# A hybrid decoder block on one core: stores moved from ScalarE's queue to SyncE's, operands made under a cap, and a recurrence paced at 9.0 products per half

## The chip, the cores and the metric

The kernel runs on one core of one Trainium2 chip. The metric is the device time of one execution in microseconds (us); the kernel before took 1485.11 us, the median of three runs (1483.97 to 1486.83). Everything is in float32. To reach that precision on TensorE, each product is made of three matmuls of fp32r parts: an operand is split into a high part (a cast on ScalarE) and a low part (source minus high part, on VectorE), and high x high, high x low and low x high are summed.

## The reference

```python
proj = x @ w_in                       # (1024, 1024) @ (1024, 7168)
q, f_pre, i_val, o_gate, pool_v, gate_a, gate_b = split(proj)
f = lb + (1 - lb) * sigmoid(f_pre);  k = 1 - f
o = hgrn2_chunked(silu(q) * 128**-0.5, k, i_val, log(f))   # 8 heads of 128, S_t = diag(f_t) S_{t-1} + k_t v_t^T
o = o * rsqrt(mean(o*o) + eps) * g * sigmoid(o_gate)
a = o @ w_a
b = per_group_linear(causal_mean(pool_v, windows 2,4,8,16) - pool_v) * pool_scale
x = LN(alpha * x + (sigmoid(gate_a) * a + sigmoid(gate_b) * b) @ w_out)
x = LN(alpha * x + (relu(x @ w_up) ** 2) @ w_down)
```

The sequence has 1024 tokens, the model 1024 columns, the MLP 4096.

## The kernel before

Every large matrix product is computed blockwise in a 2 x 2 scheme with seven products in place of eight: two output column blocks of 128 form a pair, tokens and input columns are halved, and seven products (p1 to p7 of `pair_items` and `pair`) of sums of blocks give the four output blocks. One such product is 12 matmuls of 128 x 512.

The program has these stages: the values `i_val` in rows (lines 400 to 575), the stage called `flow` here (lines 610 to 1320), the product with `w_a` and the merging of the two branches (lines 1322 to 1400), `w_out` with the first layer norm, `w_up`, and `w_down` with the second layer norm. The change touches `flow` alone.

`flow` walks through a list of 176 products (called items): 24 pairs of seven, in the order that the table `ORDER` gives (inputs of a head, output gates, pooled columns, gates), and twice four items of the pooling's small linear map, also of 12 wide matmuls each (`products`, line 898). Behind each item three things are written:

- its evacuation (`evac`): a copy from PSUM on ScalarE (`copied`, L740) or an addition on VectorE (`added`, L743). What is done with the finished block (a sigmoid and a store, for the gates) is put off by one item (`later`, `soon`);
- the making of a weight operand for a later item (`Make.high`, cast L686; `Make.low`, subtraction L689). Some operands are sums of blocks and need a VectorE operation first (`pre`: L714, L720, L721). Ten `w` tiles allow five operands to be held. `beat` makes one; then, in `while (m := next_make()): at_once(m)`, all others that have a free place are made;
- one turn of the generator `recurrence`. It works through 16 halves of heads (512 tokens of one head). In turn 0 of a half TensorE gets the outputs of the half before, the transposes of the keys (L1031) and the scores (L1038, L1049); turn 4 has more of TensorE; the elementwise preparation of the next half (`prepare`, six pieces, the last of which ends with L1022 to L1024) fills the turns between. `PER_HALF = 9.5` lets halves take 9 and 10 turns in alternation, rounded.

The pooled means (`mean`, L853 to L860) are queued as `jobs`, of which one to three are done per item. Finished gates and other blocks are written to DRAM and read again by the `w_a` stage. In `flow`, the order on TensorE, VectorE, ScalarE and SyncE is as written (`manual_schedule`); a scheduler places the instructions of the following stage between and behind. SyncE issues nearly all loads and most stores (queue SP in the profile); 48 stores stand on ScalarE's queue (16 output gates, L804; 16 gates a, L822; 16 pooled results, L924). Each engine works through its own queue in order, so an instruction that waits holds up all behind it. For PSUM there are four banks for the seven products of a pair; the accumulating product p6 needs the copy of p1 done, p5 that of p6, p4 that of p7.

In the `w_a` stage the first product needs the block of `w_a` (`loaded_blocks`, L225), its cast (L126) and the heads' outputs (`o_jobs`, splits L131 and L132).

Of the kernel before, what the change touches and what calls it, by code (L numbers as in the profile page):

```python
# [26 lines left out]
HALO = 16  # L27
LINE = 16
NW = 10
PER_HALF = 9.5  # L30
TURN_BACK = 4
TURNS_AHEAD = 3
MANY_JOBS = 4
# [18 lines left out]
def tile_hybrid_block(  # L52
# [18 lines left out]
    nc = tc.nc  # L71
# [58 lines left out]
    def split_into(t, src):  # L130
# [9 lines left out]
        out=cmask, in_=cmask, compare_op=ALU.is_ge, fill=0.0, base=0,  # L140
# [444 lines left out]
    gad = [[dram(f"ga{j}_{u}") for u in range(2)] for j in range(8)]  # L585
    pbd = [[dram(f"pb{j}_{u}") for u in range(2)] for j in range(8)]
# [32 lines left out]
    with tc.tile_pool(name="tmp", bufs=1, side="right", reuse_waits="tile") as tmp:  # L619
# [178 lines left out]
        def output_gates(h):  # L798

            def take(dst, src=False):  # L800
                def put(t):
                    s = c_late() if src else t
                    A.activation(s, t, AF.Sigmoid)
                    nc.scalar.dma_start(out=dst, in_=s)  # L804
                return put

            return pair_items(
                3 * D + h * P, 3 * D + (h + 1) * P, (c_soon, c_late, c_late),
                (take(ogd[h][0]), take(ogd[h + 1][0], True), take(ogd[h][1]), take(ogd[h + 1][1])),
            )  # L810

        def gates(j):

            p = []

            def fetch():
                p[:] = [loaded(pbd[j][u], lambda: tt("x")) for u in (1, 0)]

            def take_a(u):
                def put(t):  # L820
                    A.activation(t, t, AF.Sigmoid)
                    nc.scalar.dma_start(out=gad[j][u], in_=t)  # L822
                return put

            def take_b(u, src):
                def put(t):
                    s = c_late() if src else t
                    A.activation(s, t, AF.Sigmoid)

                    def finish():  # L830
                        V.tensor_mul(p[1 - u], p[1 - u], s)
                        nc.sync.dma_start(out=pbd[j][u], in_=p[1 - u])
                    later(finish)
                return put

            return pair_items(
                5 * D + j * P, 6 * D + j * P, (c_soon, c_late, c_late),
                (take_a(0), take_b(0, True), take_a(1), take_b(1, False)), fetch,
            )

        def pooled(g):

            j, win = 2 * g, WINDOWS[g]
# [48 lines left out]
            def take_12(ps):  # L892
# [6 lines left out]
            xw, yw, items = pair_items(  # L899
                4 * D + j * P, 4 * D + (j + 1) * P,  # L900
                (lambda: room(0, 0), lambda: room(0, 1), lambda: room(1, 1)), (take_11, take_12, take_21, lambda _: None),
            )
# [7 lines left out]
            def products(u):  # L910

                ms, ps = [part(i, u) for i in range(2)], [None, None]

                def product():
                    for i in range(2):
                        w = slice(i * P, (i + 1) * P)
                        ps[i] = ps_tile()
                        mm3(ps[i], [(mw.w[0][:, k, w], mw.w[1][:, k, w], *ms[k].w) for k in range(2)])

                def evac():  # L920
                    for i in range(2):
                        t = c_late()
                        A.activation(t, ps[i], AF.Copy, scale=pscale[:, j + i : j + i + 1])
                        nc.scalar.dma_start(out=pbd[j + i][u], in_=t)  # L924

                return Item(ms if u else [*ms, mw], product, evac)

# [295 lines left out]
        def flow(items, raws, turns, at_end):  # L1223

            makes = [m for item in items for m in item.makes]
            slots = [m for m in makes if m.slot]
            place = {m: i for i, m in enumerate(slots)}
            users = {}
            for item in items:
                for m in item.makes:  # L1230
                    users[m] = item
            state = dict(make=0, load=0)

            def free(m):
                if not m.ready():
                    return False
                if not m.slot or place[m] < NW // 2:
                    return True
                return users_of(slots[place[m] - NW // 2]).issued

            def users_of(m):
                return m.reader or users[m]

            def loads():
                while state["load"] < len(raws):
                    n = state["load"]
                    if n >= 3 and not raws[n - 3].done:
                        return
                    raws[n].load(n)
                    state["load"] += 1  # L1250

            def next_make():
                if state["make"] < len(makes) and free(makes[state["make"]]):
                    state["make"] += 1
                    return makes[state["make"] - 1]

            def at_once(m):
                m.high()
                m.low()
                loads()  # L1260

            def beat(m):
                now = list(soon)
                soon.clear()
                for do in now:
                    do()
                if m:
                    m.high()
                next(turns, None)
                for _ in range(min(len(jobs), 1 + len(jobs) // MANY_JOBS, 3)):  # L1270
                    jobs.pop(0)()
                if m:
                    m.low()
                    loads()
                if state["make"] < len(makes) and makes[state["make"]].ready():
                    makes[state["make"]].before()
                    loads()

            loads()
            for i, item in enumerate(items):  # L1280
                while state["make"] < len(makes) and any(m.w is None for m in item.makes):
                    m = next_make()
                    assert m, (i, len(jobs))
                    at_once(m)
                if i == 0:
                    while (m := next_make()):
                        at_once(m)
                item.product()
                item.issued = True
                item.evac()  # L1290
                if i in at_end:
                    jobs.extend(at_end[i])
                m = next_make()
                beat(m)
                while (m := next_make()):
                    at_once(m)
            while soon or jobs:
                beat(None)
            for _ in turns:
                pass  # L1300
# [3 lines left out]
        with tc.manual_schedule(engines={mybir.EngineType.PE, mybir.EngineType.DVE, mybir.EngineType.Activation, mybir.EngineType.SP}):  # L1304
            items, raws, pools = [], [], []
# [12 lines left out]
            n = len(items)  # L1318
# [121 lines left out]
    with tc.tile_pool(name="wo", bufs=1, side="right", reuse_waits="tile") as mp:  # L1440
        st1 = [None] * 8
        g1, b1 = ln_params(lambda: f(act_tile()).rearrange("p a b -> p (a b)"), ln1_g, ln1_b)
        for k2 in range(0, KT, 2):
            raw = raw_rows(w_out, k2, 1)
            for k in range(2):
                n = len(wo)
# [240 lines left out]
    for b in range(NBLK):  # L1687
# [3 lines left out]
        if last:  # L1691

            for ring in (dh, dw):
                t = fw.tile([P, M, 2, HALF], F32R, tag="draw", name=nm("dx"), bufs=2)
# [65 lines left out]
```

## Time and profile before

| what | value |
|---|---|
| median of three runs | 1485.11 us (1483.97 to 1486.83) |
| the profiled execution | 1482.73 us |
| its span, first to last instruction | 1480.8 us |
| granted TensorE clock, mean | 0.992 |
| TensorE busy | 1437.0 us (97%) |
| VectorE busy | 1120.1 us (76%) |
| ScalarE busy | 767.3 us (52%) |
| DMA, mean rate | 148 GB/s |

Busy time of TensorE counts from the start of a matmul to its modelled end. Matmuls overlap: one of 128 x 512 is shown with some 0.39 us, and the next starts 0.23 us later. An idle time of TensorE in the profile is therefore some 0.16 us shorter than the delay that it stands for. The profile names for each idle time the instruction that ended it, as "line of the waiting one <- engine, tile and line of what it waited for". Line numbers are those of the kernel before; in the changed kernel they are one higher up to line 1278, seven higher behind the loop.

### The profile page before, as it was taken

To read this page: it belongs to the slowest core of one execution; us is meant where nothing else is said; L and a number is where in the kernel's file an instruction comes from. 1 tells how busy PE (TensorE), PEld (TensorE's weight loads), DVE (VectorE), ACT (ScalarE), POOL (GpSimd) and SP (SyncE) were. 2 spreads that over 40 slices of the span, in tenths; PEclk is the share of its full clock that TensorE was granted. 3 is DMA by queue.
4 is the path that set the end of the run, shared out by engine and by line. 5 is a ranking of instruction groups with operands and counts; after the bars stand their busy time and mean duration, and the time that the engine had idled before them with its cause. 6 is when DMAs were issued, how large, how long until landed. Compare 5 with 4: busy or idle time off the path is not lost.

```text
span 1480.8 us, 20562 instructions
## 1 busy us (share of the span) xinstructions
PE 1437.0 (97%) x7377; PEld 1190.3 (80%) x7377; DVE 1120.1 (76%) x1822; ACT 767.3 (52%) x1397; POOL 90.9 (6%) x260
## 2 busy tenths in 40 slices
PE   9999999999999989996999999999999999999997
PEld 7888888788778778785888888888888888888886
DVE  5957888778977887757986589666666787777978
ACT  5544665765665466554542347555555533343435
POOL 0002111111111011000002100000000100000000
PEclk9999999999999999998999999999999999999999
DMA  7232241432243245559564134444464774545322
GB/s 249 79 114 86 79 135 44 141 130 86 83 161 108 64 156 159 171 174 324 177 209 167 43 129 163 142 150 150 157 227 171 272 274 133 166 131 179 132 71 114
DMA packets 164454, 218.43 MB, mean 148 GB/s; under 512 B 10976, under 2 KB 92416, under 8 KB 164352
## 3 DMA queue, kind: packets, MB, share of 16 engines
q1 hardware_dynamic: 155504, 197.96, 40.1%
q10 hardware_dynamic: 7696, 14.96, 2.8%
q0 software_dynamic: 1152, 4.19, 0.9%
q8 instruction: 58, 0.95, 0.3%
q14 instruction: 44, 0.36, 0.1%
HBM read 149.96 MB, written 67.11 MB: 147 GB/s over the span
## 4 chain that ended last, share of the span: by engine, by line
PE 83%; DVE 9%; ACT 3%; DMA 2%; issue 2%; SPq 0%; ACTq 0%; DVEq 0%
PE ps_pj L209 14%; PE ps_pj L211 13%; PE ps_pj L212 13%; PE ps_pj L1643 4%; PE ps_pj L1642 4%; PE ps_pj L1641 4%; PE ps_pj L113 2%; PE ps_pj L115 2%; PE ps_pj L114 2%; DVE x L853 1%; PE ps_tr L1643 1%; PE ps_tr L1642 1%; PE ps_tr L1641 1%; DVE w L689 1%; PE ps_sc L209 1%
## 5 line engine op out<-in xcount | busy, mean ns | idle before, releaser
L209 PE MATMUL ps_pj<-act,w 128*128 128x512 f32 x1068 | 422.8, 396 | 28.2 <-ACT w L126 12.4
L211 PE MATMUL ps_pj<-act,w 128*128 128x512 f32 x1068 | 417.5, 392 | 0.5 <-DVE act L132 0.5
L212 PE MATMUL ps_pj<-act,w 128*128 128x512 f32 x1068 | 416.8, 391 | 0.0
L209 PEld LDWEIGHTS ps_pj<-act,w 128*128 128x128 f32 x1068 | 201.9, 189 | 76.9 <-ACT c L740 15.8
L212 PEld LDWEIGHTS ps_pj<-act,w 128*128 128x128 f32 x1068 | 201.8, 189 | 42.9
L211 PEld LDWEIGHTS ps_pj<-act,w 128*128 128x128 f32 x1068 | 201.9, 189 | 41.6 <-DVE act L132 0.9
L1603 ACT CAST act<-act 128x1024 fp32r<-128x1024 f32 x66 | 66.9, 1051 | 108.7 <-issue 35.0
L686 ACT CAST w<-t 128x512 fp32r<-128x512 f32 x96 | 59.6, 621 | 82.3 <-DVE t L714 34.2
L689 DVE TENSOR_TENSOR w<-t,w 128x512 fp32r<-128x512 f32 x96 | 65.6, 683 | 39.0 <-ACT w L686 38.2
L1643 PE MATMUL ps_pj<-act,act 128*128 128x512 f32 x240 | 92.9, 389 | 0.0
L1642 PE MATMUL ps_pj<-act,act 128*128 128x512 f32 x240 | 92.9, 389 | 0.0
L1641 PE MATMUL ps_pj<-act,act 128*128 128x512 f32 x240 | 92.4, 389 | 0.0
L1604 DVE TENSOR_TENSOR act<-act,act 128x1024 fp32r<-128x1024 f32 x66 | 79.2, 1218 | 17.0 <-ACT act L1603 17.0
L689 DVE TENSOR_TENSOR w<-raw,w 128x512 fp32r<-128x512 f32 x72 | 48.5, 685 | 45.6 <-ACT w L686 44.6
L126 ACT CAST w<-t 128x512 fp32r<-128x512 f32 x74 | 46.0, 622 | 63.7 <-PE ps_pj L211 40.4
L127 DVE TENSOR_TENSOR w<-raw,w 128x512 fp32r<-128x512 f32 x71 | 48.5, 688 | 35.8 <-ACT w L126 34.7
L126 ACT CAST w<-raw 128x512 fp32r<-128x512 f32 x71 | 43.9, 622 | 55.9 <-PE ps_pj L211 29.9
L127 DVE TENSOR_TENSOR w<-t,w 128x512 fp32r<-128x512 f32 x74 | 50.7, 686 | 18.2 <-ACT w L126 18.2
L743 DVE TENSOR_TENSOR c<-c,ps_pj 128x512 f32<-128x512 f32 x64 | 43.6, 681 | 17.7 <-PE ps_pj L212 17.7
L1642 PEld LDWEIGHTS ps_pj<-act,act 128*128 128x128 f32 x240 | 45.0, 188 | 9.4
L1641 PEld LDWEIGHTS ps_pj<-act,act 128*128 128x128 f32 x240 | 45.0, 188 | 9.4
L1643 PEld LDWEIGHTS ps_pj<-act,act 128*128 128x128 f32 x240 | 45.0, 188 | 9.3
(413 smaller groups left out, 2923.6 us busy)
## 6 DMA issues: line engine op xcount, KB each, us to landing
h<-c SPq DMA_DIRECT2D x106, 256.0 KB, 2.2
raw<-in_w_in_dram SPq DMA_DIRECT2D x96, 256.0 KB, 3.3
act<-h SPq DMA_DIRECT2D x78, 256.0 KB, 2.9
draw<-in_w_down_dram SPq DMA_DIRECT2D x16, 1024.0 KB, 8.1
raw<-in_w_up_dram SPq DMA_DIRECT2D x30, 512.0 KB, 4.0
hf<-h SPq DMA_DIRECT2D x34, 256.0 KB, 2.9
og<-c ACTq DMA_DIRECT2D x16, 256.0 KB, 2.1
v<-v SPq DMA_DIRECT2D x16, 256.0 KB, 3.7
```

Source lines behind the costliest of these rows:

```text
L126: A.copy(hi, src)
L127: V.tensor_sub(lo, src, f(hi))
L209: PE.matmul(ps, wh[:, k], th, start=first and k == 0, stop=False, skip_group_check=True)
L211: PE.matmul(ps, wh[:, k], tl, start=False, stop=False, skip_group_check=True)
L212: PE.matmul(ps, wl[:, k], th, start=False, stop=k == CH - 1, skip_group_check=True)
L686: A.copy(self.w[0], self.src())
L689: V.tensor_sub(self.w[1], self.src(), f(self.w[0]))
L1603: A.copy(hi, src)
L1604: V.tensor_sub(lo, src, f(hi))
L1641: PE.matmul(ps, hh[:, w], wh, start=fresh and n == 0, stop=False, skip_group_check=True)
L1642: PE.matmul(ps, hh[:, w], wl, start=False, stop=False, skip_group_check=True)
L1643: PE.matmul(ps, hl[:, w], wh, start=False, stop=n == M - 1, skip_group_check=True)
```

## The change

Three edits in `flow`. The 48 stores move from `nc.scalar` to `nc.sync`. `PER_HALF` is 9.0, so that each half takes nine turns. And behind an item at most one operand is made beside that of `beat`, and only while fewer than four of the items that follow have all their operands (`MADE_AHEAD`).

```diff
-PER_HALF = 9.5
+PER_HALF = 9.0
+MADE_AHEAD = 4
...
-                    nc.scalar.dma_start(out=dst, in_=s)
+                    nc.sync.dma_start(out=dst, in_=s)
...
-                    nc.scalar.dma_start(out=gad[j][u], in_=t)
+                    nc.sync.dma_start(out=gad[j][u], in_=t)
...
-                        nc.scalar.dma_start(out=pbd[j + i][u], in_=t)
+                        nc.sync.dma_start(out=pbd[j + i][u], in_=t)
...
+            def ahead(i):
+                n = i + 1
+                while n < len(items) and all(m.w is not None for m in items[n].makes):
+                    n += 1
+                return n - i - 1
...
                 m = next_make()
                 beat(m)
-                while (m := next_make()):
+                if i + 1 < len(items) and ahead(i) < MADE_AHEAD and (m := next_make()):
                     at_once(m)
```

The number of instructions on each engine stays the same, but for 48 DMA issues that change from ScalarE to SyncE. The last turn of the recurrence is written behind item 175, the last one, in the kernel before, and behind item 167 in the changed one.

The first place is SyncE's queue around the end of `flow`. In the rows, `s` and `o` are sums and outputs of heads in DRAM (L1139 to L1147: the last half's), `pb` the pooled branch, `q`, `f` and `c` loads of heads' outputs, `raw<-in_w_a_dram` the blocks of `w_a`; raw_7062 is the block that the first product behind `flow` needs. Before:

```order
L832 DMA pb_1_961<-x_6931 128x512
L599 DMA q_7010<-s_0_970 128x512
L599 DMA f_7012<-s_1_971 128x512
L832 DMA pb_0_960<-x_6933 128x512
L1147 DMA s_3_977<-og_6830 128x512
L599 DMA q_7032<-s_2_972 128x512
L599 DMA gb_7195<-pb_0_946 128x512
L599 DMA f_7034<-s_3_973 128x512
L599 DMA gb_7217<-pb_0_950 128x512
L225 DMA raw_7062<-in_w_a_dram 128x4x256
```

Now:

```order
L1141 DMA s_3_969<-tA_6453 128x512
L1142 DMA og_6654<-o_0_912 128x512
L1148 DMA s_3_977<-og_6654 128x512
L600 DMA gb_7195<-pb_0_946 128x512
L600 DMA gb_7217<-pb_0_950 128x512
L226 DMA raw_7062<-in_w_a_dram 128x4x256
L226 DMA raw_7063<-in_w_a_dram 128x4x256
L226 DMA raw_7462<-in_w_a_dram 128x4x256
L833 DMA pb_1_959<-x_6780 128x512
L823 DMA ga_1_943<-c_6778 128x512
```

The recurrence's last store (s_3_977) and with it the three loads of `w_a` stood behind the last item's store (pb_0_960 of pair 7 of the gates); now they stand ahead of the stores of pair 6 (pb_1_959), and one of the moved stores (ga_1_943) follows.

The second place is TensorE's queue at the same time: w_6901 (before) is the operand of the last item of `flow`, w_6873 and w_6893 (now) those of the third and second to last, and ps_pj_7078 the bank of the first product with `w_a`. Before:

```order
L209 MATMUL ps_pj_6861<-act_762,w_6901 128x512
L211 MATMUL ps_pj_6861<-act_762,w_6901 128x512
L212 MATMUL ps_pj_6861<-act_762,w_6902 128x512
L209 MATMUL ps_pj_7078<-act_6913,w_7070 128x512
L211 MATMUL ps_pj_7078<-act_6913,w_7070 128x512
L209 MATMUL ps_pj_7093<-act_6913,w_7074 128x512
```

Now:

```order
L210 MATMUL ps_pj_6878<-act_668,w_6873 128x512
L212 MATMUL ps_pj_6878<-act_668,w_6873 128x512
L213 MATMUL ps_pj_6878<-act_668,w_6874 128x512
L210 MATMUL ps_pj_7078<-act_6925,w_7070 128x512
L212 MATMUL ps_pj_7078<-act_6925,w_7070 128x512
L210 MATMUL ps_pj_6901<-act_460,w_6893 128x512
```

The products with `w_a` began behind the last item; now their first two matmuls stand two items earlier.

The third place is ScalarE's queue at the last of the four spots where a pooled map's items (L923, evacuation with a scale, and its store L924) are followed by a new pair, whose first product's copy is L740. Before:

```order
L923 ACTIVATE c_5707<-ps_pj_5693,prm 128x512
L924 DMA pb_1_959<-c_5707 128x512
L923 ACTIVATE c_5710<-ps_pj_5700,prm 128x512
L924 DMA pb_1_961<-c_5710 128x512
L686 CAST w_5714<-t_5687 128x512
L686 CAST w_5730<-t_5728 128x512
L740 COPY c_5747<-ps_pj_5734 128x512
```

Now:

```order
L924 ACTIVATE c_5798<-ps_pj_5784,prm 128x512
L924 ACTIVATE c_5801<-ps_pj_5791,prm 128x512
L687 CAST w_5805<-t_5778 128x512
L741 COPY c_5831<-ps_pj_5818 128x512
L687 CAST w_5833<-t_5816 128x512
```

Two stores and one of two casts no longer stand between the pooled evacuations and the copy; the second cast comes behind it. At the other three such spots there is one cast in place of two as well; at two of them the copy has the recurrence's squares or scalings (L1105, L1113) ahead of it now.

## The prediction

> **What bounds the kernel now.** I read the page's busy times first, then TensorE (PE) by stage, then who PE waited for.
>
> ```profile
> span 1480.8 us, 20562 instructions
> PE 1437.0 (97%) x7377; PEld 1190.3 (80%) x7377; DVE 1120.1 (76%) x1822; ACT 767.3 (52%) x1397; POOL 90.9 (6%) x260
> ```
>
> PE is idle for 1480.8 - 1437.0 = 43.8 us. The change removes no matmul, so it can only win from these waits and from time at a lowered clock. The stages, in the view by windows (busy us and count of each engine, then granted clock, DMA share, GB/s), are `flow`, the first moments of the `w_a` stage, its next 25 us, and the rest:
>
> ```profile
> 99.70:673.50 573.80, 557.41 (x3454) 462.99 (x3452) 447.03 (x869) 334.29 (x721) 68.86 (x211) 0.99 0.38 121
> 673.50:692.00 18.50, 6.10 (x15) 4.82 (x16) 12.92 (x21) 8.73 (x16) 0.00 (x0) 0.63 1.01 348
> 692.00:716.70 24.70, 24.10 (x108) 19.60 (x106) 21.51 (x35) 16.52 (x30) 0.00 (x0) 1.00 0.76 263
> 716.70:1480.80 764.10, 753.82 (x3352) 623.28 (x3352) 566.53 (x777) 359.04 (x547) 19.21 (x14) 1.00 0.46 158
> ```
>
> The change touches `flow` (16.4 us idle) and what follows at once (12.4 us and a clock of 0.63). The last row's code is the same in both kernels. Whom PE waited for:
>
> ```profile
> PE ps_pj L209 <- ACT w L126: 12.4, 1, 12.4
> PE ps_pj L209 <- ACT c L740: 12.0, 9, 3.6
> PE ps_pj L209 <- DVE f L743: 1.8, 2, 1.0
> ...
> PE ps_tr L1031 <- DVE tC L1022: 1.4, 2, 1.0
> ```
>
> One wait of 12.4 us at the seam, nine waits in `flow` for ScalarE's (ACT) copies out of PSUM, and little else.
>
> **The change, part by part.**
>
> *The seam.* PE's timeline there:
>
> ```profile
> 672.88 0.39 PE L211 MATMUL ps_pj<-act,w 128*128 128x512 f32 x1
> 673.11 0.39 PE L212 MATMUL ps_pj<-act,w 128*128 128x512 f32 x1
> 685.90 0.80 PE L209 MATMUL ps_pj<-act,w 128*128 128x512 f32 x1 [12.40 <-ACT w L126]
> ...
> 687.35 0.63 PE L211 MATMUL ps_pj<-act,w 128*128 128x512 f32 x1
> 687.77 0.63 PE L212 MATMUL ps_pj<-act,w 128*128 128x512 f32 x1
> ```
>
> Starts are 0.23 us apart ahead of the hole and 0.42 behind it. From start to start the hole is 12.79 us, 12.6 more than 0.23. The 15 matmuls counted up to 692.0 come at the halved clock and cost some 15 x 0.2 = 3.0 more. What PE waits for is the cast of the first block of `w_a`, and that waits for its load, which SyncE (SP) issues so late:
>
> ```profile
> 676.01 0.44 SPq L832 DMA_DIRECT2D pb<-x  x1
> 676.90 0.32 SPq L1147 DMA_DIRECT2D s<-og  x1
> ...
> 679.48 1.49 SPq L225 DMA_DIRECT2D raw<-in_w_a_dram  x3
> ```
>
> The loads stand behind the last item's store and the recurrence's last store, since the recurrence's last turn comes with the last item. With nine turns it comes with item 167, eight products or 8 x 12 x 0.23 = 22 us ahead of the end, and the order shows the three loads right behind its store, ahead of the stores of the second to last pair. A load of this kind lands in 5.6 us:
>
> ```profile
> raw<-in_w_a_dram SPq DMA_DIRECT2D x8, 512.0 KB, 5.6
> ga<-ga SPq DMA_DIRECT2D x16, 256.0 KB, 5.4
> og<-c ACTq DMA_DIRECT2D x16, 256.0 KB, 2.1
> pb<-x SPq DMA_DIRECT2D x16, 256.0 KB, 2.2
> ```
>
> So the blocks should be there over 10 us early, and PE's queue has the first matmuls of `w_a` two items ahead of the end of `flow`. The hole and the halved clock go: -15.6. What is late next is data. From 673.5 to 716.7 the transfers moved 18.5 x 348 + 24.7 x 263 KB per us, 12.9 MB. Of it 1.8 MB (three blocks of 512 KB and the last store of 256 KB) come earlier now; 11.1 MB stay. PE needs 43.2 - 15.6 = 27.6 us for the products in this stretch; 11.1 MB take 31.9 us at 348 GB/s and 42.2 at 263. By the first rate 4.3 us of wait come back, by the second 14.6. The faster rate is the one seen while PE waited for transfers, and some loads of heads' outputs get free behind the earlier stores too: I take 3.1. **Term: -12.5**, with ends -15.6 and -1.0.
>
> *At most two operands per product, stores off ACT.* Four of the nine waits for a copy come where a pooled map's items precede a new pair:
>
> ```profile
> 188.36 0.50 PE L209 MATMUL ps_pj<-act,w 128*128 128x512 f32 x1 [0.19 <-ACT c L740]
> ...
> 287.97 0.50 PE L209 MATMUL ps_pj<-act,w 128*128 128x512 f32 x1 [1.39 <-ACT c L740]
> ...
> 413.57 0.50 PE L209 MATMUL ps_pj<-act,w 128*128 128x512 f32 x1 [1.67 <-ACT c L740]
> ...
> 544.43 0.50 PE L209 MATMUL ps_pj<-act,w 128*128 128x512 f32 x1 [3.63 <-ACT c L740]
> ```
>
> Together 6.9 us. ACT's timeline shows why for the longest:
>
> ```profile
> 540.29 0.33 ACTq L924 DMA_DIRECT2D pb<-c  x1
> 540.66 0.62 ACT L686 CAST w<-t 128x512 fp32r<-128x512 f32 x1 [0.40 <-ACT c L923]
> 543.27 0.62 ACT L686 CAST w<-t 128x512 fp32r<-128x512 f32 x1 [2.00 <-DVE t L714]
> 543.80 0.58 ACT L740 COPY c<-ps_pj 128x512 f32<-128x512 f32 x1
> ```
>
> The second operand's cast waits 2.0 us for VectorE (DVE), and the copy stands behind it. The order puts this cast behind the copy now, and the two stores ahead of it, each 0.4 us from one ACT operation to the next, are gone. 2.0 + 0.6 + 0.8 = 3.4 of the 3.63 us go. The same is done at the other three spots. Two of them have the recurrence's squares in the way instead, but these come with PE's own extra work of that turn. The clock, by windows:
>
> ```profile
> 504.00:512.00 8.00, 6.17 (x21) 4.61 (x20) 7.65 (x18) 1.80 (x4) 0.00 (x0) 0.79 0.00 0
> 542.00:550.00 8.00, 5.57 (x17) 4.43 (x18) 7.32 (x15) 4.30 (x10) 0.00 (x0) 0.79 0.60 193
> 411.00:418.00 7.00, 5.33 (x23) 4.07 (x23) 6.13 (x13) 3.48 (x10) 0.10 (x1) 1.00 0.27 90
> ```
>
> Behind the wait of 3.63 us (second row) the clock loses 0.21 x 8 = 1.7 us; that goes with it. So up to 8.6 us can go; I take **-7**, with ends -8.6 and 0.
>
> The Trainium skill ("TensorE: Matmul & The Clock Gate", "What's actually happening") says that the clock is halved after an idle window of about 3.4 us. The trace differs: the row 504 to 512 shows the loss with an idle time of only 1.8 us in it, while 1.67 us (third row) cost none. By the page's rule every wait under 3.4 us that the new order makes is free of it; by the first row each of 1.8 us can cost 1.7, and only the wide end of my range has room for several.
>
> *The recurrence at 9.0.* Per product there is 9.5 / 9.0 = 1.056 times its work until item 167 and none behind. This costs only where DVE is full:
>
> ```profile
> 360.00:415.00 55.00, 50.82 (x290) 41.08 (x289) 50.14 (x107) 30.43 (x63) 8.25 (x23) 1.00 0.25 78
> 490.00:533.00 43.00, 38.70 (x231) 31.40 (x230) 39.78 (x86) 22.01 (x48) 5.37 (x17) 0.96 0.20 60
> ```
>
> These are the two stretches in which the pooled means of the wide windows are worked off; DVE is busy for 91% and 93%. Were all its work the recurrence's and every us of it on the path, it would add 0.056 x (50.1 + 39.8) = 5.0 us; elsewhere DVE has room (447 of 574 us over all of `flow`). The lower end is 0. I take half: **+2.5**. The other waits of `flow`, 16.4 - 6.9 = 9.5 us, I leave as they are; the halves start elsewhere among the pairs now, so each can move, and I give them 4 us either way.
>
> *48 stores on SP.* ACT is freed of 48 issues; outside of the spots above it has room (334 of 574 us), so nothing is counted. SP gets 48 issues of 0.3 to 0.4 us and waits at each until ACT has written the tile. Behind them stand raw loads, the recurrence's loads and the `pb` loads. How tight these are shows in who waited for a landing in `flow`:
>
> ```profile
> DVE og L1146 <- DMA og<-o: 3.2, 3, 1.7
> ...
> ACT w L686 <- DMA raw<-in_w_in_dram: 0.5, 1, 0.5
> ```
>
> A raw load was waited for once in 96; a store would have to hold SP for many products to be felt. L1146, the last sum of a head, is tight: its load is issued in turn 7, and nine turns leave it one product where ten left two. Four times up to 1.7 us on DVE, which PE feels only in a full stretch: **0**, with +2 in the range. The Trainium skill ("DMA: Bandwidth & Descriptors", "Issuing engines are not separate DMA queues") says that transfers interleave on the same 16 engines whoever starts them, and that several issuers save only issue time. The rows above agree: 2.1 us from ACT and 2.2 from SP to landing. By it the move as such brings nothing but ACT's time, and the sum has nothing else for it.
>
> **Sum:** -12.5 - 7 + 2.5 = -17 us against the profiled execution's 1482.7 (span 1480.8 and 1.9 around it), so 1465.7. The median of the runs is 1485.1, 2.4 above that execution; set off from it the forecast is **1468.1 us**.
>
> **The rivals.**
>
> *The transfers become the seam's bound.* For: 348 GB/s at a share of 1.01 in the row from 673.5, and 5.4 us to landing for `ga<-ga`. Against: a part of that rate was the late loads themselves. At 263 GB/s the seam's gain is 1.0: -1.0 - 7 + 2.5, 1479.6.
>
> *DVE is the bound in the full stretches and the waits only move.* For: 93% busy. The gains at the four spots are eaten by DVE's lag: -12.5 + 0 + 5.0 = -7.5, 1477.6.
>
> *Slower: PE waits for the last piece of `prepare` at the start of each half.* Place: the transposes L1031 of turn 0. With ten turns the last piece has a spare product, with nine it is written one product ahead of them, for all halves and not about every other one. It decides when DVE is over one product (2.7 us) behind at a half's end. At 2.7 us for 15 halves it costs 40 us, so 1468.1 + 40 = 1508; at a third of that the gain is nearly gone (1481). Against: halves of nine turns are there already, and the whole wait at L1031 was 1.4 us.
>
> *The change does not do what it says:* the loads of `w_a` are held by something else, such as space that the recurrence's tiles free, or PE, with two `w_a` matmuls ahead of its last items, stops there instead. Then the hole only moves: -7 + 2.5, 1480.6.
>
> *Better:* the smaller waits go as well (9.5 us and 1.7 of clock, half of it): 1462.5; with all, 1456.9.
>
> **How the numbers follow.** Forecast (1464 to 1474) 0.55, better 0.11, transfers 0.10, DVE 0.11, hole only moved 0.05, slower by L1031 0.08. A measurement of this kernel can tell about 0.2%, 3 us, from no change; below 1482.1 is faster. Faster are the first four (0.87) and 0.02 of the hole's case: 0.89. Same: the other 0.03 of it and 0.02 of L1031's, at a third of its price: 0.05. Slower: 0.06. The range reaches from all small waits gone to the hole only moved, with some us of moved waits: 1455 to 1481.
>
> **What would show it.** PE's wait for L127 (L126 before) gone or under 3 us, with the clock at 1.00 behind the seam and the `w_a` loads issued over 10 us ahead of the last product of `flow`. The waits for L741 at the four spots gone. Waits for L1032 (L1031 before) few, under 4 us in sum. DVE over 90% busy in the two full stretches, with PE's waits there up by under 5 us. Wrong would be: one wait over 5 us at the seam, waits for L1032 at most halves, or PE's waits for DVE and ACT in `flow` above 16.4 us in sum.

## The result, and the profile after

The changed kernel takes **1485.39 us** (median of 12 runs, 1484.29 to 1488.61), the kernel before 1484.3 us in the same comparison (12 runs, 1482.36 to 1487.02): a ratio of 1.0009, 95% interval 1.0000 to 1.0018. The change made no difference that this measurement can tell; 1468.1 us had been forecast, and a range up to 1481.

The page of the changed kernel, span and busy times:

```profile
span 1484.8 us, 20578 instructions
PE 1441.0 (97%) x7377; PEld 1192.6 (80%) x7377; DVE 1119.6 (75%) x1822; ACT 760.9 (51%) x1397; POOL 81.3 (5%) x260
```

The same stretches of time as in the prediction (busy us and count of each engine, then clock, DMA share, GB/s):

```profile
99.70:673.50 573.80, 548.53 (x3393) 455.34 (x3392) 438.12 (x855) 321.90 (x708) 59.23 (x211) 0.98 0.36 116
673.50:692.00 18.50, 15.76 (x62) 12.88 (x63) 12.98 (x22) 10.12 (x19) 0.00 (x0) 0.91 0.87 303
692.00:716.70 24.70, 24.13 (x106) 19.63 (x105) 22.34 (x38) 16.86 (x31) 0.00 (x0) 1.00 0.86 292
```

Read the counts of TensorE's instructions. In the stretch that held the hole of 12.4 us PE now issues 62 in place of 15, at a clock of 0.91 in place of 0.63: the hole is gone. But up to 673.5 us it issued 3393 in place of 3454: what the seam gives was taken ahead of it (but for 1.8 us that belong to a wait at the seam, below). Whom PE waited for says by whom (us in sum, times, longest):

```profile
PE ps_pj L210 <- ACT c L741: 14.7, 6, 6.3
PE ps_tr L1032 <- DVE tC L1023: 9.1, 7, 3.1
PE ps_pj L210 <- DVE f L744: 4.2, 2, 2.3
```

No row for L127, the cast of `w_a` (12.4 us before); these three sum to 28.0 us, where the waits of `flow` made 16.4 us before. The waits for a copy were nine with 12.0 us and are six with 14.7, the longest of them 6.3; those for the last piece of `prepare` (L1032) went from 1.4 to 9.1 us. Of the 28.0 us, 18.0 lie in and just behind the two full stretches of the pooled means (374 to 403 and 495 to 543 us); before, those made 6.8 us without the four spots. The clock went with them. Four of the stretches in which it fell:

```profile
400.00:408.00 8.00, 5.67 (x18) 4.24 (x17) 6.70 (x15) 3.73 (x8) 0.00 (x0) 0.79 0.36 106
500.00:512.00 12.00, 8.90 (x82) 7.18 (x81) 6.90 (x17) 5.61 (x19) 0.20 (x2) 0.72 0.14 46
528.00:540.00 12.00, 7.66 (x24) 6.03 (x24) 11.51 (x28) 3.93 (x8) 0.00 (x0) 0.72 0.40 124
608.00:616.00 8.00, 8.00 (x81) 6.58 (x80) 3.84 (x7) 5.04 (x17) 0.00 (x0) 0.79 0.80 241
```

(1 - 0.79) x 8 = 1.7 us and (1 - 0.72) x 12 = 3.4 us of clock are lost in such a stretch, 10.2 us in these four; before there were two of 1.7 us in `flow`.

The seam itself is not quite free. SyncE's queue and VectorE there, then ScalarE, then PE:

```profile
662.44 0.32 SPq L1142 DMA_DIRECT2D og<-o  x1
...
669.33 1.48 SPq L226 DMA_DIRECT2D raw<-in_w_a_dram  x3
```

```profile
667.22 0.69 DVE L1147 TENSOR_TENSOR og<-og,tA 128x512 f32<-128x512 f32 x1 [4.27 <-DMA og<-o]
...
669.04 0.68 DVE L744 TENSOR_TENSOR c<-c,ps_pj 128x512 f32<-128x512 f32 x1
```

```profile
669.75 0.64 ACT L822 ACTIVATE c<-c 128x512 f32<-128x512 f32 x1 [5.62 <-DVE c L744]
...
675.61 0.58 ACT L741 COPY c<-ps_pj 128x512 f32<-128x512 f32 x1
```

```profile
676.24 0.50 PE L210 MATMUL ps_pj<-act,w 128*128 128x512 f32 x1 [4.56 <-ACT c L741]
```

The three loads of `w_a` that were issued at 679.48 before are issued at 669.33 now, 10 us earlier. But the load for the last head's last sum (`og<-o`) is issued at 662.44 and waited for until 667.22; VectorE stands still for 4.27 us with an addition (L744) behind it, and ScalarE waits 5.62 us for that. Between this and the copy that PE needs, ScalarE has two more casts that wait for sums, 1.56 and 1.52 us: from L822 to the copy it is 5.9 us (669.75 to 675.61). In e7 below, where the limit is five and one cast fewer stands there, it is 3.1 us (656.70 to 659.78), and VectorE waits 2.21 us for the same load. So the 4.56 us by which the copy comes late are made by the load and by the operands together. The clock behind it:

```profile
676.00:684.00 8.00, 7.76 (x27) 6.26 (x28) 5.45 (x9) 4.49 (x9) 0.00 (x0) 0.79 1.02 362
```

Another 1.7 us are lost there.

### The profile page after: what moved, and what is told of

The parts are those of the page before. It is cut to its first block, busy times and chain, and to the rows that moved or that the text cites. A ratio compares the mean times of both kernels' runs of the same rounds, so it can differ in the third digit from the quotient of the medians.

```text
span 1484.8 us, 20578 instructions
## 1 busy us (share of the span) xinstructions
PE 1441.0 (97%) x7377; PEld 1192.6 (80%) x7377; DVE 1119.6 (75%) x1822; ACT 760.9 (51%) x1397; POOL 81.3 (5%) x260
## 4 chain that ended last, share of the span: by engine, by line
PE 81%; DVE 12%; ACT 3%; issue 2%; DMA 1%; SPq 0%; DVEq 0%; ACTq 0%
PE ps_pj L210 13%; PE ps_pj L212 12%; PE ps_pj L213 12%; PE ps_pj L1649 4%; PE ps_pj L1648 4%; PE ps_pj L1650 4%; PE ps_pj L114 2%; PE ps_pj L115 2%; PE ps_pj L116 2%; DVE w L690 2%; DVE x L854 2%; PE ps_tr L1649 1%; PE ps_tr L1648 1%; PE ps_tr L1650 1%; PE ps_sc L210 1%
## 5 line engine op out<-in xcount | busy, mean ns | idle before, releaser
L210 PE MATMUL ps_pj<-act,w 128*128 128x512 f32 x1068 | 423.2, 397 | 19.6 <-ACT c L741 14.7
L687 ACT CAST w<-t 128x512 fp32r<-128x512 f32 x96 | 59.3, 618 | 95.2 <-DVE t L721 32.6
L127 ACT CAST w<-t 128x512 fp32r<-128x512 f32 x74 | 45.9, 622 | 61.8 <-PE ps_pj L212 40.0
L127 ACT CAST w<-raw 128x512 fp32r<-128x512 f32 x71 | 44.1, 622 | 52.4 <-PE ps_pj L212 27.8
L744 DVE TENSOR_TENSOR c<-c,ps_pj 128x512 f32<-128x512 f32 x64 | 43.5, 680 | 23.1 <-PE ps_pj L213 23.1
```

The costliest lines, as they stand in the source:

```text
L127: A.copy(hi, src)
L210: PE.matmul(ps, wh[:, k], th, start=first and k == 0, stop=False, skip_group_check=True)
L687: A.copy(self.w[0], self.src())
```

## The experiments

Every ratio is to the kernel before in the same comparison (median 1484.7 us for e1 to e4, 1484.6 for e5 to e8, 1485.2 for e9 to e12, 1484.9 for e13 to e16), with its 95% interval. The first theory was that the pace of the recurrence makes both the gain at the seam and the loss in `flow`; its rival, that the cap makes the loss.

### Each edit alone: e1, e2, e3, and all without the pace: e4

```diff
# e1: the kernel before
-PER_HALF = 9.5
+PER_HALF = 9.0
# e2: the kernel before
-                while (m := next_make()):
+                if i + 1 < len(items) and ahead(i) < MADE_AHEAD and (m := next_make()):
# e3: the kernel before, at three places
-nc.scalar.dma_start(
+nc.sync.dma_start(
# e4: the changed kernel
-PER_HALF = 9.0
+PER_HALF = 9.5
```

> The kernel before with PER_HALF = 9.0 alone. Theory (the pace of the recurrence makes both the gain at the seam and the loss in flow): the wait of 12.4 us for the cast of w_a is gone, the waits for the last piece of prepare (L1031 here) rise from 1.4 to about 9 us, ScalarE's waits for the differences of weight blocks (L720, L721) rise, PE's waits in flow are well above 16.4 us, and the time is within 3 us of the kernel before (1481 to 1488 us). Rival (the cap on operands made ahead is what costs in flow): the seam's gain of about 13 us stays whole here, the time is 1470 to 1474 us, and the waits in flow are those of before.

> The kernel before with the cap on operands made ahead alone (recurrence at 9.5, stores on ScalarE). Theory (the pace): the four waits where a pooled map precedes a new pair (6.9 us) get shorter, the wait at the seam stays at 12 us, the waits for L1031 stay at 1 to 2 us; 3 to 8 us faster, 1476 to 1481 us. Rival (the cap): PE's waits in flow go up by over 8 us with the seam unchanged, 1492 us or more.

> The kernel before with the 48 stores on SyncE's queue alone. Theory (the pace): within 2 us of the kernel before, 1482 to 1487 us, with about 1.6 us less at the four spots and the waits for the last sums' load (og<-o, 3.2 us) unchanged. Rival (late loads behind the moved stores cost): the waits for og<-o and tH<-o rise as in the changed kernel (7.4 and 3.4 us), and 3 us or more are lost.

> The changed kernel with PER_HALF back at 9.5 (cap and stores stay). Theory (the pace): the wait of about 12 us at the seam is back, the four waits behind the pooled maps are gone, the waits for L1032 fall to 1 to 2 us; 1476 to 1480 us, the gain of the cap and the stores alone. Rival (the cap): seam's wait back and the flow's waits as long as in the changed kernel, about 1497 us.

| kernel | median us | ratio (95%) | waits in `flow` | wait for the cast of `w_a` |
|---|---|---|---|---|
| e1, pace alone | 1479.11 | 0.9958 (0.9945 to 0.9970) | 22.1 | none |
| e2, cap alone | 1493.45 | 1.0058 (1.0045 to 1.0070) | 19.4 | 15.3 |
| e3, stores alone | 1483.56 | 0.9991 (0.9983 to 1.0000) | 16.1 | 14.9 |
| e4, cap and stores | 1489.49 | 1.0030 (1.0019 to 1.0041) | 16.9 | 15.9 |

(Waits of PE from 100 us on, in us, summed from the view of waits; the kernel before has 16.4 and 12.4.)

The pace alone gains 5.6 us, the stores 1.1 us, **the cap alone loses 8.8 us**. The sum, +2.1, is what the changed kernel shows, +1.1, within the intervals. The first theory falls as far as the loss goes: it is the cap's. The rival holds but for two things: in e1 it wanted the seam's gain whole, so the pace too costs something in `flow`; and for e4 it wanted about 1497 us.

### Which half of the cap: e5, e6, and without it: e7, e8

The cap says two things: at most two operands per product, and none beyond the first once four products ahead have theirs. With a limit of five the second never holds, and the operands are made as before but for one at each of four places, where three were made behind one product and it now comes one product later.

```diff
# e5: as e2, and e7: the changed kernel
-MADE_AHEAD = 4
+MADE_AHEAD = 5
# e6: as e2
-                if i + 1 < len(items) and ahead(i) < MADE_AHEAD and (m := next_make()):
+                while i + 1 < len(items) and ahead(i) < MADE_AHEAD and (m := next_make()):
# e8: e1 and e3 together
```

> The kernel before with the cap's limit raised from four to five products ahead, which leaves of the cap only 'at most two per product' and moves an operand at four places alone, behind the four pairs of a pooled map's items. Theory (the limit of four is what costs: it puts off the operands of each pair by one product, so that t3 and t2, which share one tile and are made in sequence by VectorE and ScalarE, fall into one product): the four waits of 0.2 to 3.6 us behind the pooled maps get shorter, ScalarE's waits for L721 (L720 before) stay below those of the cap alone (29.7 us), 2 to 6 us faster than before, 1479 to 1483 us. Rival (two at most per product is itself too little, the operands come late whatever the limit): 3 us or more slower, 1488 us or more.

> The kernel before with the limit of four products ahead alone, and as many operands per product as it allows. Theory (the limit): 6 to 12 us slower than before, 1491 to 1497 us, with ScalarE's waits for L721 at about 30 us as in the cap alone. Rival (two at most is what costs): within 3 us of before.

> The changed kernel with MADE_AHEAD = 5 in place of 4. Theory (the limit): the 8.8 us that the cap alone cost go, and the gains of the pace (5.6 us) and the stores (1.1 us) are seen, with 0 to 4 us more at the four spots: 1474 to 1479 us. Rival (the loss comes from the recurrence's density and the cap only adds to it in the kernel with 9.5): 1482 us or more.

> The kernel before with PER_HALF = 9.0 and the 48 stores on SyncE, without the cap. Theory (the edits add up): -5.6 and -1.1 us, 1477 to 1479 us. Rival (the moved stores delay the loads that the recurrence at 9.0 needs): 1481 us or more, with VectorE's waits for og<-o at 7 us and over.

| kernel | median us | ratio (95%) |
|---|---|---|
| e5, two at most | 1487.32 | 1.0017 (1.0006 to 1.0027) |
| e6, limit of four | 1492.29 | 1.0054 (1.0040 to 1.0067) |
| e7, the change with a limit of five | 1474.47 | 0.9931 (0.9915 to 0.9946) |
| e8, pace and stores | 1476.29 | 0.9936 (0.9919 to 0.9953) |

**One digit, 4 for 5, is worth 10.9 us** (1485.39 against 1474.47). The limit of four loses 7.7 us by itself; "two at most" loses 2.7 alone and makes no difference that can be told beside the pace (e7 against e8). At the four places for which I had counted on it, it gains nothing: PE's waits there are 9.8 us in e5's profile (1.41, 1.89, 2.31 and 4.15) and were 6.9 before. ScalarE in e5 at the last of them:

```profile
546.27 0.62 ACT L687 CAST w<-t 128x512 fp32r<-128x512 f32 x1 [0.40 <-ACT c L924]
548.88 0.62 ACT L687 CAST w<-t 128x512 fp32r<-128x512 f32 x1 [1.99 <-DVE t L715]
549.41 0.58 ACT L741 COPY c<-ps_pj 128x512 f32<-128x512 f32 x1
```

The same two casts ahead of the copy as before, and the same 2 us of wait. Three operands behind one product were made five products earlier, in the pair ahead of the pooled map's items; here there are two, which the rule allows. In the changed kernel it is the limit that lets only one be made and so clears the place.

### How the limit costs: e9 and e10

At nearly every pair the kernel before makes two operands behind the fourth product, `t0` and `b21` of the next pair, both plain blocks; then one each: `t3`, `t2`, `t1`, `t4`, `b22`. With the limit `b21` is put off by one product, and `t3` with it, so that it falls behind the sixth product, where `t2` is made too: the product with two operands is now that of **`t3` and `t2`**. These share one tile: cast and subtraction of `t3` must be done before L721 adds to it, and only then comes the cast of `t2`. ScalarE's waits for such sums, in the kernel before, then in the changed one:

```profile
ACT w L686 <- DVE t L714: 34.2, 23, 4.3
ACT w L686 <- DVE t L721: 31.1, 19, 5.2
ACT w L686 <- DVE t L720: 6.5, 5, 2.3
```

```profile
ACT w L687 <- DVE t L721: 32.6, 22, 4.7
ACT w L687 <- DVE t L715: 30.2, 26, 2.5
ACT w L687 <- DVE t L722: 29.0, 17, 6.4
```

The row for the sum `t2` (L720 before, L721 after) goes from 6.5 us at 5 places to 32.6 at 22. It is 29 to 33 us in the four kernels with the limit so far and 5 to 8 us in the six without it. What that does to PE is seen by laying the same half of the recurrence side by side, the changed kernel and e7 (VectorE):

```profile
599.40 0.41 DVE L1013 TENSOR_TENSOR tD<-tE,rT 128x256 f32<-128x256 f32 x1
599.73 0.68 DVE L690 TENSOR_TENSOR w<-t,w 128x512 fp32r<-128x512 f32 x1
600.45 0.69 DVE L721 TENSOR_TENSOR t<-t,raw 128x512 f32<-128x512 f32 x1
601.90 0.69 DVE L690 TENSOR_TENSOR w<-t,w 128x512 fp32r<-128x512 f32 x1 [0.76 <-ACT w L687]
602.51 0.68 DVE L832 TENSOR_TENSOR x<-x,c 128x512 f32<-128x512 f32 x1
603.12 0.68 DVE L715 TENSOR_TENSOR t<-raw,raw 128x512 f32<-128x512 f32 x1
...
606.80 0.68 DVE L1023 TENSOR_TENSOR tC<-tE,ek 128x512 f32<-128x512 f32 x1
```

```profile
592.00 0.42 DVE L1013 TENSOR_TENSOR tD<-tE,rT 128x256 f32<-128x256 f32 x1
592.34 0.69 DVE L690 TENSOR_TENSOR w<-t,w 128x512 fp32r<-128x512 f32 x1
592.94 0.68 DVE L715 TENSOR_TENSOR t<-raw,raw 128x512 f32<-128x512 f32 x1
...
597.22 0.68 DVE L1023 TENSOR_TENSOR tC<-tE,ek 128x512 f32<-128x512 f32 x1
```

From L1013 to L1023, the last piece of `prepare`, it is 7.40 us and 5.22: the sum L721, its subtraction, and the 0.76 us in which VectorE waits for the cast between them, stand in the row. PE's wait for that piece:

```profile
607.63 0.30 PE L1032 MATMUL ps_tr<-ident,tC 128*128 128x128 f32 x1 [1.78 <-DVE tC L1023]
```

In e7 it is 0.33 us at 598.05, and the clock stays up, while the changed kernel loses 1.7 us of it behind this wait (the row 608 to 616 above). The longest wait of `flow` shows the same, first in the changed kernel, then in e7:

```profile
532.34 0.79 PE L210 MATMUL ps_pj<-act,w 128*128 128x512 f32 x1 [6.25 <-ACT c L741]
```

```profile
523.05 0.80 PE L210 MATMUL ps_pj<-act,w 128*128 128x512 f32 x1 [4.12 <-ACT c L741]
```

Ahead of both VectorE works off the same list, but in the changed kernel the sum L721, a wait of 0.74 us and a second subtraction stand in it, 2.2 us in all.

Two experiments take the place apart:

```diff
# e9: the changed kernel; sum = whether an operand has a difference or sum of blocks
-                if i + 1 < len(items) and ahead(i) < MADE_AHEAD and (m := next_make()):
+                n = state["make"]
+                if n < len(makes) and not makes[n].sum and ahead(i) < MADE_AHEAD and (m := next_make()):
# e10: the kernel before; late = 1 for t3, 0 for the others
-                return users_of(slots[place[m] - NW // 2]).issued
+                return users_of(slots[place[m] - NW // 2 + m.late]).issued
```

> The changed kernel, limit of four and all, but the second operand of a product is made only if it is no sum of blocks, so that t3 and t2 of a pair fall into two products, one operand each, and t2, t1, t4 and b22 come one product later still. Theory (the two sums in one product cost): most of the 10.9 us between the changed kernel (1485.4) and the one with a limit of five (1474.5) comes back, 1473 to 1479 us, with ScalarE's waits for L721 at under 12 us (32.6 in the changed kernel). Rival (that the operands come later is what costs, wherever they fall): 1485 us or more.

> The kernel before with one thing changed: t3 waits until the place of t2 is free too, so that both are made behind the same product. All other operands are made where they were. Theory (the two sums in one product cost): as the limit alone, 5 to 10 us slower, 1490 to 1495 us, with ScalarE's waits for L720 at about 30 us (6.5 in the kernel before). Rival (the lateness of all operands): within 3 us of the kernel before.

e9 took 1475.42 us, 0.9941 (0.9929 to 0.9953); e10 1493.43 us, 1.0060 (1.0048 to 1.0072). ScalarE's waits for the sum `t2` in e9 and in e10:

```profile
ACT w L687 <- DVE t L721: 10.4, 13, 1.6
```

```profile
ACT w L686 <- DVE t L720: 37.4, 22, 5.2
```

In e9 most operands come later still than in the changed kernel, one behind each product, and 10 us are back. In e10 nothing is late but `t3`, by one product, and 8.2 us are lost, as much as by the whole cap. So it isn't lateness: **it is that `t3` and `t2` are made behind one product, the second of them a sum that has to be added, cast and subtracted on the spot.** Whether it takes the tile that they share was not tried. At the four spots the kernel before makes `t2` and `t1` behind one product; `t1` has a tile of its own, and still its cast waits 2.0 us for its difference (the row at 543.27 in the prediction) and PE up to 3.63.

### What the pace costs: e11 and e12

```diff
# e11: as e7
-PER_HALF = 9.0
+PER_HALF = 9.25
# e12: as e7
+LONGER = (7, 8, 11, 12)
-                turns = round(at + PER_HALF) - round(at)
+                turns = round(at + PER_HALF) - round(at) + (n in LONGER)
```

> The changed kernel with the limit of five and PER_HALF = 9.25: four halves of ten turns, in the third, sixth, eleventh and fourteenth place, and the recurrence ends four products later than at 9.0, five before the end of flow. Theory (what the recurrence at 9.0 still costs in flow comes from the stretches in which VectorE is full of the pooled means): ten turns elsewhere help little there, 1472 to 1478 us, about as with 9.0 (1474.5). Rival (it is the waits for the last piece of prepare, which fall by a quarter of the halves): 1470 us or less.

> The changed kernel with the limit of five and PER_HALF = 9.0, but ten turns for the four halves that run beside the pooled means of the two wide windows. The same number of turns in all as with 9.25. Theory (VectorE's full stretches): PE's waits between 380 and 560 us (about 12 us at 9.0) fall by half or more, 1466 to 1471 us, 3 us or more below the kernel with 9.25. Rival (where the ten turns are makes no difference): the same as with 9.25 within 2 us.

e11 took 1479.07 us, 0.9962 (0.9951 to 0.9974), 1.1 us above its range and 4.6 us more than e7; e12 took **1470.61 us, 0.9904 (0.9891 to 0.9917)**. The same number of turns in the same kernel, and 8.5 us between them. Two of the rows of PE's waits in e11, then in e12 (whose lines are one higher):

```profile
PE ps_pj L210 <- ACT c L741: 13.6, 8, 3.5
PE ps_tr L1032 <- DVE tC L1023: 5.3, 6, 1.5
```

```profile
PE ps_pj L211 <- ACT c L742: 7.2, 5, 2.2
...
PE ps_tr L1033 <- DVE tC L1024: 1.5, 1, 1.5
```

With all rows it is 23.7 us in e11 and 17.8 in e12; in both the wait for the cast of `w_a` is back, with 3.0 and 3.6 us, since the recurrence ends four products later. Where the long halves lie counts. My number for how was wrong, though: from 380 to 560 us the waits fell from 12.1 us in e7 to 10.7, not by half, and in sum they are nearly the same (18.4 and 17.8 us). What differs is the clock: summed over the stretches in which it was low, idle time included, e7's profile lost 10.2 us and e12's 3.4, which is more than the 3.9 us between their times. The longest wait beside the means, ahead of 523 us, is an example; the stretch around it in e7, then in e12:

```profile
520.00:532.00 12.00, 8.44 (x24) 6.38 (x24) 11.59 (x26) 3.86 (x8) 0.00 (x0) 0.72 0.37 110
```

```profile
520.00:532.00 12.00, 11.29 (x56) 9.18 (x55) 9.83 (x20) 5.25 (x9) 3.33 (x10) 1.00 0.22 65
```

### Without the pooled means: e13, e14, e15, and the two remedies joined: e16

```diff
# e13: the kernel before; e14: e10; e15: e7
-                    for lev in range(g + 1):
+                    for lev in range(0):
# e16: e9 and e12 together
```

> The kernel before without the additions of the pooled means (the loop over the levels does no step, so that the pooled branch is computed from the values alone): VectorE has some 40 us less to do, nearly all of it in the stretches from 360 to 415 and 490 to 533 us. It is the base of the next two. Theory (VectorE's fullness in these stretches makes most of PE's waits in flow): PE's waits in flow, 16.4 us in the kernel before, fall by half or more, 4 to 10 us faster than before. Rival (the order of the operands makes them, however full VectorE is): under 3 us faster.

> The same without the means' additions, and t3 put off behind the same product as t2, which cost 8.2 us with the means in. Theory (two sums in one product cost because they meet a full VectorE): 0 to 3 us slower than the kernel without the means. Rival (the chain from t3's cast over the subtraction and the sum t2 to its cast costs by its own length): 6 us or more slower than it.

> The changed kernel with the limit of five and without the means' additions (the recurrence at 9.0). Theory (the recurrence at 9.0 costs only where VectorE is full): the whole gain at the seam shows, 13 us or more faster than the kernel before without the means, and PE's waits in flow stay under 8 us. Rival (the last piece of prepare is late at nine turns whatever else VectorE does): waits at L1032 of 5 us and more remain, and under 10 us are gained.

> The kernel with the second operand only where it is no sum, and with ten turns for the four halves beside the pooled means of the wide windows: the two versions that were fastest, joined. Theory (both take work off VectorE where it is full, and partly the same waits): 1468 to 1472 us, about as the longer halves alone (1470.6). Rival (two causes that add up): 1466 us or less.

| kernel | median us | ratio to the kernel before (95%) |
|---|---|---|
| e13, before without the means' additions | 1469.91 | 0.9901 (0.9885 to 0.9916) |
| e14, e13 with `t3` put off | 1476.23 | 0.9946 (0.9930 to 0.9961) |
| e15, e7 without the means' additions | 1453.35 | 0.9789 (0.9774 to 0.9805) |
| e16, e9 and e12 | 1469.81 | 0.9901 (0.9883 to 0.9918) |

PE's waits in e13, without the row for `w_a`, and then all of `flow`'s in e15:

```profile
PE ps_pj L209 <- ACT c L740: 5.8, 5, 2.3
...
PE ps_tr L1031 <- DVE tC L1022: 0.3, 1, 0.3
```

```profile
PE ps_pj L210 <- ACT c L741: 4.3, 3, 3.0
...
PE ps_tr L1032 <- DVE tC L1023: 1.9, 2, 1.5
```

Three things follow. First, with 33 us less on VectorE (1087.2 in place of 1120.1) PE's waits in `flow` fall from 16.4 to 6.1 us: its fullness makes most of them, and the gain (15 us) was larger than I expected. Second, putting `t3` off still costs 6.3 us (e14 against e13), nearly the 8.2 of e10; here my theory fell and the rival's chain, which costs by its own length, holds. Third, nine turns per half, with the stores and "two at most", gain 16.6 us without the means (e15 against e13) and 10.2 with them (e7): 6.4 us are at most what the recurrence at 9.0 loses to the means (1.1 us of them may be the wait for the cast of `w_a`, which is 13.5 us in e13 and 12.4 in the kernel before), and the waits for the last piece of `prepare`, 4.8 us in e7, are 1.9 in e15.

e16 can't be told from e12: the two remedies don't add up. That they take away the same waits is likely, but not shown. Both beat the kernel before and the changed one by 1%.

## Why the prediction was wrong

*The seam* was right as a mechanism: the last turn, the loads and PE's first products with `w_a` come as the order showed, and the wait for L127 is gone. Of the forecast 3.1 us to come back, 4.56 us came, and 1.7 of clock, but not as late data for `w_a`: VectorE waits for the load of the last sum, `og<-o`, the very row that the prediction named (L1146) and priced at nothing, and the limit of four puts one more cast in the way. Without that limit it is data, and of the forecast size: 3.04 us in e1, where VectorE waits 3.32 us for a block of `w_a`, and 2.61 in e7 and 3.20 in e8, where ScalarE waits 1.79 us for a load of a head's output. The 1.7 to 3.4 us of clock behind these waits were not in the forecast. Where the means are out, the pace with the stores and "two at most" brings 16.6 us (e15 against e13), so -12.5 was hardly too much for the seam.

*"At most two operands per product, stores off ACT"*, priced at -7 with ends of -8.6 and 0, **is the step that failed**. With the stores it came out at +4.8 us at 9.5 products per half (e4) and at +6.3 at 9.0 (1485.39 against e1's 1479.11): 12 to 13 us from the forecast, and outside its ends. The four waits did go in the changed kernel. But I read the order where the four waits were, took the rule that cleared them to be "two at most", and held all other operands to be unmoved; the limit of four moves two operands at nearly every pair of `flow`, and puts `t3` and `t2` behind one product. That alone costs 8.2 us (e10), and undoing it gives 10 back (e9). The rows for it were in the view of waits: 34.2 and 31.1 us of ScalarE's waits for `t`. They say what an operand that is a sum costs its engine; I never asked where such operands go.

*The recurrence at 9.0*, priced at +2.5 (0 to 5.0), is a term that was mis-sized: it is up to 6.4 us. It was reckoned as VectorE's own time alone, and the clock was left out of it. In e1 the waits in `flow` are 5.7 us above the kernel before's, 3.0 of them near the seam, and by the clock 8.5 us are lost ahead of the seam in place of 3.4. The pace as a whole was to gain 12.5 - 2.5 = 10.0 us and gained 5.6 (e1). These 4.4 us and the 13.3 of the step that failed make up the miss, 17.3 us from 1468.1 to 1485.39, but for 0.4.

*The stores*: 0 forecast, -1.1 measured (e3), its interval up to none.

*The other waits of `flow`*, left as they were with 4 us either way, are where it all shows: 9.5 us before, 28.0 - 4.6 = 23.4 us now, without the four that went.

Of the rivals, "slower by the last piece of `prepare`" came in part: 9.1 us in seven waits, not 40; the limit had made it worse (4.8 in e7, 4.9 in e1). "DVE is the bound and the waits only move" was the nearest in kind, but the waits moved for the order of the operands, and nothing in the prediction would have put the time where it was. Of the signs of being wrong that I had named, one showed: waits in `flow` above 16.4 us. Of those that would have borne the forecast out, two failed: the waits for L1032 stayed under 4 us no more (9.1), and those at the two full stretches went up by 11 us and not by under 5.

Open: in a single profile each, the wait for the cast of `w_a` is 14.6 to 15.9 us in e2, e3, e4, e6 and e10, and 12.4 in the kernel before; why was not followed. What the limit costs is therefore not all lost in `flow`: in e10's profile PE ends its last product of `flow` 5.9 us later than before (679.4 and 673.5 us), and the rest of its 8.8 us comes behind that. The stores gain 1.1 us alone, 2.8 beside the pace (e8 against e1) and 4.0 beside the cap (e4 against e2), and no run says why. Why "two at most" alone loses 2.7 us and none beside the pace was not settled either, though the waits at the four spots grew by about as much (2.9 us); part of e5's profile is a stretch of low clock in the first 20 us that no edit touches.

## What to carry to other kernels

When a change limits how far ahead work is made, list the order at every repetition of the loop and not only at the places that it is meant for; and look at which two pieces now fall together: here a second operand that is itself a sum cost 8 us over the kernel, and with that sum made one product later the loss was gone. Price a wait with the clock: in e7 the waits were 18.4 us and the stretches of low clock lost 10.2. And a pace that is right on the average can be set where it hurts: the same four long halves were worth 8.5 us more beside the stretches in which VectorE is full.

## What the runs showed of the hardware

The clock falls for stretches of 3.4 us or a multiple (a loss of 1.7 or 3.4 us in the rows above), but not behind a fixed length of wait. In the changed kernel a wait of 1.78 us (607.63 us) was followed by one such stretch, and these two were followed by none:

```profile
394.82 0.50 PE L210 MATMUL ps_pj<-act,w 128*128 128x512 f32 x1 [3.09 <-ACT c L741]
...
542.12 0.50 PE L210 MATMUL ps_pj<-act,w 128*128 128x512 f32 x1 [1.87 <-DVE f L744]
```

The Trainium skill ("TensorE: Matmul & The Clock Gate", "What's actually happening") says that the activity is judged in windows of about 3.4 us that run freely and don't start with the work. By that the place of a wait in its window decides beside its length, and the trace agrees: 1.78 us were enough once and 3.09 were not.

The edges of the low stretches show such windows directly. In the changed kernel the clock falls at 403.9, 502.9, 530.2, 608.7 and 676.95 us, which is 29, 8, 23 and 20 times 3.413 us from one to the next; in the kernel before it falls at 507.3 and 544.85, 11 times 3.413 apart, on a grid that lies elsewhere. Three windows of the changed kernel's grid: one with a part of the wait of 3.09 us, the one ahead of the fall at 608.7, and the one behind that fall:

```profile
390.24:393.65 3.41, 1.49 (x7) 0.89 (x5) 3.34 (x9) 1.22 (x3) 1.87 (x8) 1.00 0.07 20
...
605.28:608.70 3.42, 1.64 (x57) 1.29 (x55) 2.60 (x6) 0.73 (x2) 0.00 (x0) 1.00 0.82 258
608.70:612.11 3.41, 3.41 (x20) 2.79 (x15) 1.90 (x4) 1.18 (x3) 0.00 (x0) 0.50 0.67 201
```

The wait of 3.09 us was cut in two by the edge at 393.65. In all profiles with a fall between 100 and 700 us, a window of their grid begun at full clock in which PE was shown busy for less than 1.45 of its 3.41 us was always followed by half the clock, and one with more than 1.7 never; in between both occur, as these rows show. So a wait need not fill a window, as the prediction read from its row 504 to 512: a wait between some 1.8 and 3.1 us costs 1.7 us more in some places and nothing in others, and by this a change that shifts all later work by a microsecond can turn either on. As the grid lies elsewhere in each profile, what one profile loses by the clock is one draw.
